# Small 64-row products that run over all 128 rows, and a mask product in float32r

## The chip, the core and the metric

The kernel runs on one core of one Trainium2 chip. The metric is the device time of one launch in microseconds (us), the median of three runs.

## What is computed

Two transformer blocks over one sequence of 512 tokens with 1024 features. All matrices are float32.

- First block, two layers: stick-breaking attention (16 heads of 64 features) and a squared-relu MLP; then retention (4 heads) and another such MLP; then a norm.
- Second block: a SwiGLU network, a mixer that runs two branches side by side, and a second SwiGLU network. One branch of the mixer is attention over the 128 keys that an index picks for each query (8 index heads and 8 attention heads of 64 features, two key/value heads). The other is an mLSTM (4 heads with queries and keys of 64 features).

Four kinds of product in it sum over just 64 features. The first of these lines is one of them, with the mask that belongs to it; the third is the index:

```
z = jnp.einsum('bhqd,bhkd->bhqk', qb, kp) * scale
mask = s_idx < t_idx
logits = jnp.einsum('bqhd,bsd->bqhs', iq_blk, ik)
```

## The kernel before

A float32 operand x is kept as two float32r tiles, hi and lo, with x = hi + lo; the class `Pair` holds the two. A product of two such operands is three TensorE products (`mm3`, lines 114 to 116): hi by lo, lo by hi, and hi by hi. Weights come from HBM in panels on SyncE's DMA queue; ScalarE rounds each to hi (line 197) and VectorE subtracts to get lo (line 198). Nearly every weight product moves 512 columns (the tokens).

Where the sum runs over 64 features, 64 rows of the array would stand empty, and `mm2` (lines 118 to 123) uses them. The stationary tile, `stack`, has hi of a head in one half of the 128 partitions and lo in the other. One product over all 128 rows then gives hi by hi and lo by hi at once (line 123, its moving tile has hi in both halves). What is missing is hi by lo, and line 122 makes it with a product over the 64 rows of hi alone: `stack[sl]` against `rhs.lo[sl]`, where `sl` is the head's half.

`mm2` is called in four places: `sb_z` (scores of stick-breaking attention, 64 calls), `select` (the index scores, 24), `attend_head` (attention scores, 32) and `weights` inside `mlstm` (16). That is 136 pairs of a 64-row and a 128-row product. They move 256, 384 or 512 columns.

The moving tiles are made in four places. `doubled` (line 142) makes them for the 16 stick-breaking heads, two heads at a time; the two heads share one lo tile, each has its own half. `ev` inside `mqk` (line 960) does the same for the mLSTM. The index keys (`ik_done`) and attention keys (`k_done`) already have lo in both halves.

In `sb_z` each score block also gets its mask from TensorE: a product of an identity and a constant `far` (-1e30 where the key is not before the query), 128 columns, added in PSUM (line 568). Both constants are bfloat16.

TensorE's order is woven: the generator `filler` yields weight products, and `pump` puts four `mm3` of them between two score blocks; in the mixer `weave` puts one step of the index, mLSTM or attention chain after every so many `mm3`. The instructions are then laid out by a scheduler, which may shift single ones. All tiles called h are taken from one heap of 70 buffers. VectorE, ScalarE and GpSimd (POOL) each run their own instructions in order. POOL does little: it clears the front columns of some tiles (lines 594 and 595) and cuts triangles (line 667).

Of the kernel before, what the change touches and what calls it, by code (L numbers as in the profile page):

```python
# [23 lines left out]
# tiles of the heap, buffers of the weights, and how far apart the woven chains put their steps  # L24
# [26 lines left out]
# pieces of the first panel  # L51
# [5 lines left out]
# [128, 512] views of one attention head's score blocks: (s-block, first t, columns in the bank)  # L57
# [6 lines left out]
# columns in front that hold only s > t  # L64
# [3 lines left out]
class Pair:  # L68
    """A float32 operand as two float32r tiles, x = hi + lo."""
# [8 lines left out]
class Builder:  # L78
# [39 lines left out]
    def mm2(self, ps, stack, rhs, sl, first, last):  # L118
        """Products over 64 partitions: stack holds hi in the partitions sl and lo in the other half, rhs is a
        Pair whose hi lies in both halves and whose lo lies (at least) in sl."""  # L120
        mm = self.nc.tensor.matmul
        mm(ps, stack[sl], rhs.lo[sl], start=first, stop=False)  # L122
        mm(ps, stack, rhs.hi, start=False, stop=last)  # L123

    def stack(self, f, scale=None):
        """[128, n], two heads of 64 features -> for each head a tile with hi in its half and lo in the other."""
# [15 lines left out]
    def doubled(self, f):  # L142
        """[128, n], two heads of 64 features -> for each head a Pair: hi in both halves, lo in its own."""
        nc = self.nc
        lo = self.h(F32R)
        out = []
        for b in range(2):
            t = self.h(F32R)
            a = slice(64 * b, 64 * b + 64)
            o = slice(64 - 64 * b, 128 - 64 * b)  # L150
            nc.scalar.activation(t[a], f[a], AF.Copy)
            nc.vector.tensor_tensor(lo[a], f[a], t[a].bitcast(F32), ALU.subtract)
            nc.vector.tensor_copy(t[o], t[a])
            out.append(Pair(t, lo))
        return out
# [8 lines left out]
    def panels(self, name, idxs):  # L164
        """Panels in the order of their use; each is one DMA and one or two subpanels."""
# [20 lines left out]
    def prep(self, ahead=AHEAD):  # L186
        """Split the next subpanel unless `ahead` of them wait already."""
# [15 lines left out]
    def next(self, name):  # L203
        """The next subpanel, a Pair."""
        assert self.subs[self.pos][0] == name, (self.subs[self.pos], name)
        while self.prep_at <= self.pos:
            self.prep(1)
        p = self.ready.pop(self.pos)
        self.pos += 1
        return p  # L210
# [11 lines left out]
    def g_tokens(self, name, X, done):  # L222
        """out [t, 512] = x W for the four token tiles; done(tt, psum)."""
# [11 lines left out]
    def g_tokens_turn(self, name, X, done):  # L235
        """The same, some token tiles after the other."""
# [12 lines left out]
    def later(self, f, *a, lag=None):  # L249
        """f(*a) after some more products."""  # L250
# [19 lines left out]
    def weave(self, main, chains=()):  # L270
        """Emit main's products, with a step of each chain [generator, period] every so many of them."""
# [9 lines left out]
    def rsqrt_col(self, v):  # L281
        """v -> v ** -0.5 for a few columns: three Newton steps from the exponent's half."""
# [12 lines left out]
    def spread(self, ps, cols, p=128):  # L295
        """cols(tt): [128, p] whose columns repeat (token on partition) -> ps [p, 512], token on the free axis."""
# [3 lines left out]
    def rows_of(self, ps, src, rhs, n=1, at=0, step=None, first=True, last=True):  # L300
        """Sums over src's partitions weighted by rhs [p, n], per token: ps[:, at + tt * step : + n]."""
# [17 lines left out]
    def mean_sq(self, box):  # L319
        """[128, 4] PSUM columns: sums of squares of the tokens."""  # L320
# [16 lines left out]
    def norm_soon(self, st, box, n1=N1, n2=N2):  # L337
        """Put the reciprocal norm into st["rcol"] and st["R"] while the first products run."""
# [8 lines left out]
    def gain_in(self, x, g):  # L347
        """hi/lo of x * g (g one value per partition)."""
# [7 lines left out]
    def setup(self):  # L356
# [9 lines left out]
        # ntri[j, s] = -1 where j >= s  # L366
# [6 lines left out]
        # far[s, c] = -1e30 where s >= c  # L373
# [4 lines left out]
        self.far = self.const("far", [128, 128], BF16)  # L378
        nc.vector.tensor_copy(self.far, far)
        # 1/64 within each half of the partitions  # L380
# [4 lines left out]
        # gains: one column per 128 features  # L385
# [9 lines left out]
    def mlp(self, layer, hh, X, box, nxt):  # L395
        """hh += relu(rms(hh) W_up)^2 W_down, X = hh * gain; calls nxt(m) when hh[m] is final."""
# [164 lines left out]
    def sb_z(self, q, k, head, ch, Z, i):  # L561
        sl = slice(64 * (head % 2), 64 * (head % 2) + 64)
        w = WIDTH[ch]
        z = self.ps("o" if ZB and i % 5 == 4 else "z")
        for j, t0, c0, c1 in CHUNKS[ch]:
            self.mm2(z[:, c0:c1], k[:, j * 128:(j + 1) * 128], q[:, t0:t0 + c1 - c0], sl, c0 == 0, False)
            d = c0 + j * 128 - t0
            self.nc.tensor.matmul(z[:, d:d + 128], self.identb, self.far, start=False, stop=c1 == w)
        Z[i] = z

    def sb_l1(self, Z, L, hc, i):
        """softplus(z), part one: ln(1 + exp(-|z|))."""
# [17 lines left out]
    def chunk(self, ch):  # L590
        """A Pair for a chunk, with zeros in the front columns."""
# [6 lines left out]
    def sb_tri(self, Z, L, A, hc, i):  # L598
        """z - sum of the softplus of the keys from s to t - 1, and its exponential."""
# [48 lines left out]
    def stack_values(self, vs, ps, scale):  # L648
        """[128, 512], eight heads of 64 -> two tiles of four heads, each 64 columns of hi and 64 of lo."""
# [7 lines left out]
    def mm_values(self, ps, v, a, first, last):  # L657
        """v [keys, 64 of hi, 64 of lo]: what v.lo brings lands in the partitions 64 to 127 of ps."""
# [4 lines left out]
    def keep(self, e, ch):  # L663
        """Zero where s > t."""
# [148 lines left out]
    def ffn(self, which, hh, X, st, nxt):  # L813
        """hh += (silu(x W_gate) * (x W_up)) W_down / 2, with x = X * st["R"]."""
# [17 lines left out]
        def main():  # L832
            for gi, grp in enumerate((range(0, 8), range(8, 16), range(16, 22))):
# [11 lines left out]
                if tail:  # L845
                    # the last tile in parts, so that little is left behind the last product
# [13 lines left out]
    def head_norm(self, x, gcol, done, p=128):  # L860
        """done(x [p, 512] * rsqrt(mean over each 64 partitions of x^2 + eps) * gcol), some products later."""
# [26 lines left out]
    def mixer(self, hh, X, box, nxt):  # L888
# [10 lines left out]
        # small projections: index key 0:64, input gate 64:68, index weights 68:76, forget gate 96:100  # L899
# [38 lines left out]
        # mLSTM operands  # L938
# [14 lines left out]
        def mqk():  # L953
            w = self.next("mqk")
            for h in range(4):
# [4 lines left out]
                def ev(ps=ps, h=h):  # L960
                    a = slice(64 * (h % 2), 64 * (h % 2) + 64)
                    o = slice(64 - 64 * (h % 2), 128 - 64 * (h % 2))
                    hi = self.h(F32R)
                    nc.scalar.activation(hi[a], ps[a], AF.Copy, scale=0.0625)
                    nc.scalar.activation(hi[o], ps[a], AF.Copy, scale=0.0625)
                    if h % 2 == 0:
                        MQ["lo"] = self.h(F32R)
                    lo = MQ["lo"]
# [40 lines left out]
        # attention operands  # L1009
# [131 lines left out]
    def topk_weights(self, gw):  # L1141
        """Index weights of tokens 128..511 as columns: [128, 24], eight to a query block."""
# [10 lines left out]
    def select(self, IQ, IK, late, BIAS):  # L1153
        """Attention bias [128, 512] of query blocks 1 to 3: 0 at the TOPK chosen keys, FAR elsewhere."""
# [5 lines left out]
        for tb in (1, 2, 3):  # L1160
            n = 128 * (tb + 1)
            sc = SC[tb] = self.h()
            for h in range(8):
                w = iw[:, (tb - 1) * 8 + h:(tb - 1) * 8 + h + 1]
                sl = slice(64 * (h % 2), 64 * (h % 2) + 64)
                ps = self.ps("z")
                self.mm2(ps[:, :n], IQ[h // 2][h % 2][:, tb * 128:(tb + 1) * 128], IK[:, 0:n], sl, True, True)
# [20 lines left out]
    def attend_all(self, AQ, KD, AV, BIAS, YA, choose, st):  # L1188
        """The eight heads' attention, query block by query block and group by group."""
# [23 lines left out]
    def attend_head(self, tb, g, hg, AQ, KD, BIAS, rq):  # L1213
# [5 lines left out]
        sl = slice(64 * (h % 2), 64 * (h % 2) + 64)  # L1219
        ps = self.ps("z")  # L1220
        self.mm2(ps[:, :w], AQ[h // 2][h % 2][:, tb * 128:(tb + 1) * 128], KD[g][:, 0:w], sl, True, True)
# [36 lines left out]
    def gates(self, gw, fgx, out):  # L1258
        """From the gate rows: exponent columns per (query block, key block), rows M, columns exp(-(F + M))."""
# [65 lines left out]
    def mlstm(self, MQ, MK, MV, gates, SO, YB):  # L1325
# [6 lines left out]
        # rows 32 h: sums of the weights, sums of num^2  # L1332
# [12 lines left out]
        def weights(h, ch):  # L1345
            o = slice(64 - 64 * (h % 2), 128 - 64 * (h % 2))
# [391 lines left out]
```

## Time and profile before

| | |
|---|---|
| median of three runs | 2569.13 us (2567.39 to 2570.67) |
| profiled execution, first to last instruction (span) | 2567.1 us |
| TensorE products busy (PE) | 2550.2 us, 99% of the span |
| TensorE weight loads busy (PEld, beside PE) | 2071.6 us, 81% |
| VectorE busy (DVE) | 1461.0 us, 57% |
| ScalarE busy (ACT) | 971.2 us, 38% |
| GpSimd busy (POOL) | 23.4 us, 1% |

The profile gives no time of its own for the profiled execution beside its span; the median of the runs is 2.0 us above that span. Products overlap in the records (one of 512 columns is shown 390 ns long, and the next one starts 230 ns after it), so the busy share of PE says that products follow each other without a break, and not how long one holds the array. That is read from the distance between starts. In the rows, "64*128 64x256" means that the stationary tile has 64 rows and 128 columns, and that 64 rows of 256 columns move.

### The profile page before, as it was taken

To read this page: it belongs to the slowest core of one execution; us is meant where nothing else is said; L and a number is where in the kernel's file an instruction comes from. 1 tells how busy PE (TensorE), PEld (TensorE's weight loads), DVE (VectorE), ACT (ScalarE), POOL (GpSimd) and SP (SyncE) were. 2 spreads that over 40 slices of the span, in tenths; PEclk is the share of its full clock that TensorE was granted. 3 is DMA by queue.
4 is the path that set the end of the run, shared out by engine and by line. 5 is a ranking of instruction groups with operands and counts; after the bars stand their busy time and mean duration, and the time that the engine had idled before them with its cause. 6 is when DMAs were issued, how large, how long until landed. Compare 5 with 4: busy or idle time off the path is not lost.

```text
span 2567.1 us, 28649 instructions
## 1 busy us (share of the span) xinstructions
PE 2550.2 (99%) x11511; PEld 2071.6 (81%) x11511; DVE 1461.0 (57%) x2386; ACT 971.2 (38%) x1428; POOL 23.4 (1%) x102
## 2 busy tenths in 40 slices
PE   9999999999999999999999999999999999999999
PEld 7777788888888888888888888888777778888887
DVE  7777754445555545645446644446788767543443
ACT  6676622223333323322223322223555454322221
POOL 0000000000000000000000000000000000000000
PEclk9999999999999999999999999999999999999999
DMA  4112022222222222222222222223121112222221
GB/s 166 57 42 99 33 99 99 99 99 99 94 85 85 86 82 103 79 94 92 97 99 99 96 93 91 99 90 107 63 82 66 61 55 82 99 99 98 93 86 68
DMA packets 35277, 225.58 MB, mean 88 GB/s; under 512 B 4036, under 2 KB 4420, under 8 KB 9800
## 3 DMA queue, kind: packets, MB, share of 16 engines
q1 hardware_dynamic: 34992, 223.69, 25.3%
q8 instruction: 91, 1.49, 0.2%
q14 instruction: 42, 0.34, 0.0%
q10 hardware_dynamic: 152, 0.06, 0.0%
HBM read 221.63 MB, written 2.10 MB: 87 GB/s over the span
## 4 chain that ended last, share of the span: by engine, by line
PE 97%; DVE 2%; ACT 1%; issue 1%; DMA 0%; SPq 0%; DVEq 0%
PE ps_m L114 28%; PE ps_m L115 28%; PE ps_m L116 28%; PE ps_z L122 2%; PE ps_z L123 2%; PE ps_z L116 1%; PE ps_z L114 1%; PE ps_z L115 1%; PE ps_z L614 1%; PE ps_z L615 1%; PE ps_o L298 1%; PE ps_o L305 1%; PE ps_m L660 0%; PE ps_m L661 0%; PE ps_z L886 0%
## 5 line engine op out<-in xcount | busy, mean ns | idle before, releaser
L114 PE MATMUL ps_m<-h,whi 128*128 128x512 f32 x3050 | 1195.4, 392 | 0.9 <-DVE h L920 0.4
L115 PE MATMUL ps_m<-h,wlo 128*128 128x512 f32 x3050 | 1189.1, 390 | 0.0
L116 PE MATMUL ps_m<-h,whi 128*128 128x512 f32 x3050 | 1188.2, 390 | 0.0
L197 ACT ACTIVATE whi<-raw 128x1024 fp32r<-128x1024 f32 (+2 forms) x417 | 437.5, 1049 | 1294.4 <-PE ps_m L116 1205.6
L116 PEld LDWEIGHTS ps_m<-h,whi 128*128 128x128 f32 x3050 | 573.4, 188 | 120.1
L114 PEld LDWEIGHTS ps_m<-h,whi 128*128 128x128 f32 x3050 | 573.9, 188 | 118.4 <-issue 3.1
L115 PEld LDWEIGHTS ps_m<-h,wlo 128*128 128x128 f32 x3050 | 573.7, 188 | 113.5 <-issue 1.2
L198 DVE TENSOR_TENSOR wlo<-raw,whi 128x1024 fp32r<-128x1024 f32 (+2 forms) x417 | 503.8, 1208 | 192.6 <-ACT whi L197 192.1
L159 ACT ACTIVATE h<-h 128x512 fp32r<-128x512 f32 (+1 forms) x172 | 107.9, 630 | 102.8 <-DVE h L405 27.7
L409 DVE TENSOR_TENSOR h<-h,ps_m 128x512 f32<-128x512 f32 x64 | 44.0, 687 | 170.4 <-PE ps_m L116 170.4
L160 DVE TENSOR_TENSOR h<-h 128x512 fp32r<-128x512 f32 (+1 forms) x172 | 116.3, 682 | 14.9 <-ACT h L159 14.2
L404 DVE TENSOR_TENSOR h<-ps_m,h 128x512 f32<-128x512 f32 x64 | 44.2, 691 | 139.3 <-PE ps_m L116 138.5
L823 DVE TENSOR_TENSOR h<-ps_m,h 128x512 f32<-128x512 f32 x43 | 29.7, 691 | 127.8 <-PE ps_m L116 127.8
L828 DVE SCALAR_TENSOR_TENSOR h<-ps_m,h 128x512 f32<-128x512 f32 x47 | 32.5, 692 | 118.9 <-PE ps_m L116 118.9
L820 DVE TENSOR_TENSOR h<-ps_m,h 128x512 f32<-128x512 f32 x42 | 29.0, 691 | 91.7 <-PE ps_m L116 91.1
L114 PE MATMUL ps_m<-wlo,h 128*128 128x512 f32 x176 | 70.2, 399 | 1.7 <-DVE wlo L198 1.7
L115 PE MATMUL ps_m<-whi,h 128*128 128x512 f32 x176 | 69.0, 392 | 0.0
L116 PE MATMUL ps_m<-whi,h 128*128 128x512 f32 x176 | 68.7, 391 | 0.0
L122 PE MATMUL ps_z<-h 64*128 64x256 f32 (+2 forms) x124 | 52.6, 427 | 2.2 <-ACT h L972 2.2
L122 PEld LDWEIGHTS ps_z<-h 64*128 64x128 f32 x124 | 22.6, 184 | 37.5 <-issue 21.7
L123 PE MATMUL ps_z<-h 128*128 128x256 f32 (+2 forms) x124 | 52.7, 429 | 0.0
L405 DVE SCALAR_TENSOR_TENSOR h<-h 128x512 f32<-128x512 f32 x64 | 44.3, 692 | 2.1
(286 smaller groups left out, 2028.9 us busy)
## 6 DMA issues: line engine op xcount, KB each, us to landing
raw<-gu SPq DMA_DIRECT2D x44, 1024.0 KB, 4.7
raw<-up SPq DMA_DIRECT2D x32, 1024.0 KB, 4.8
raw<-dn SPq DMA_DIRECT2D x32, 1024.0 KB, 4.8
raw<-fd SPq DMA_DIRECT2D x16, 1024.0 KB, 4.7
raw<-sbqk SPq DMA_DIRECT2D x8, 1024.0 KB, 4.8
raw<-retqk SPq DMA_DIRECT2D x8, 1024.0 KB, 4.7
raw<-retv SPq DMA_DIRECT2D x8, 1024.0 KB, 4.8
raw<-retg SPq DMA_DIRECT2D x8, 1024.0 KB, 4.8
```

What stands on the lines that cost most here:

```text
L114: mm(ps, lhs.hi, rhs.lo, start=first, stop=False, skip_group_check=skip)
L115: mm(ps, lhs.lo, rhs.hi, start=False, stop=False, skip_group_check=skip)
L116: mm(ps, lhs.hi, rhs.hi, start=False, stop=last, skip_group_check=skip)
L122: mm(ps, stack[sl], rhs.lo[sl], start=first, stop=False)
L123: mm(ps, stack, rhs.hi, start=False, stop=last)
L159: self.nc.scalar.activation(p.hi, x, AF.Copy)
L160: self.nc.vector.tensor_tensor(p.lo, x, p.hi.bitcast(F32), ALU.subtract)
L197: nc.scalar.activation(hi[:, a:b], r[:, a:b], AF.Copy)
L198: nc.vector.tensor_tensor(lo[:, a:b], r[:, a:b], hi[:, a:b].bitcast(F32), ALU.subtract)
L404: nc.vector.tensor_tensor(z, ps, st["R"], ALU.mult)
L405: nc.vector.scalar_tensor_tensor(z, z, 0.0, z, ALU.max, ALU.mult)
L409: nc.vector.tensor_tensor(hh[m], hh[m], ps, ALU.add)
```

## The change

1. `mm2` no longer takes the half `sl`: both products run over all 128 rows. For the first to give hi by lo alone, the moving lo tile is zero in the half where the stationary tile holds lo; where lo stood in both halves already (index keys, attention keys), the sum now has lo by lo as well.
2. `doubled` and `ev` in `mqk` make one lo tile for each head instead of one for two, and POOL clears its other half (20 new instructions in all: 16 for the stick-breaking heads, 4 for the mLSTM).
3. `far` and the identity of the mask product become float32r (the identity is now called `identr`).

Comments and docstrings are dropped as well, which shifts line numbers by a few: line 122 becomes 123, line 123 becomes 124, line 568 becomes 569.

```diff
-    def mm2(self, ps, stack, rhs, sl, first, last):
+    def mm2(self, ps, stack, rhs, first, last):
         mm = self.nc.tensor.matmul
-        mm(ps, stack[sl], rhs.lo[sl], start=first, stop=False)
+        mm(ps, stack, rhs.lo, start=first, stop=False)
         mm(ps, stack, rhs.hi, start=False, stop=last)
...
     def doubled(self, f):
         nc = self.nc
-        lo = self.h(F32R)
         out = []
         for b in range(2):
-            t = self.h(F32R)
+            t, lo = self.h(F32R), self.h(F32R)
             a = slice(64 * b, 64 * b + 64)
             o = slice(64 - 64 * b, 128 - 64 * b)
+            nc.gpsimd.memset(lo[o].bitcast(F32), 0.0)
             nc.scalar.activation(t[a], f[a], AF.Copy)
...
-        self.far = self.const("far", [128, 128], BF16)
+        self.far = self.const("far", [128, 128], F32R)
         nc.vector.tensor_copy(self.far, far)
...
-            self.mm2(z[:, c0:c1], k[:, j * 128:(j + 1) * 128], q[:, t0:t0 + c1 - c0], sl, c0 == 0, False)
+            self.mm2(z[:, c0:c1], k[:, j * 128:(j + 1) * 128], q[:, t0:t0 + c1 - c0], c0 == 0, False)
             d = c0 + j * 128 - t0
-            self.nc.tensor.matmul(z[:, d:d + 128], self.identb, self.far, start=False, stop=c1 == w)
+            self.nc.tensor.matmul(z[:, d:d + 128], self.identr, self.far, start=False, stop=c1 == w)
...
-                    hi = self.h(F32R)
+                    hi, lo = self.h(F32R), self.h(F32R)
+                    nc.gpsimd.memset(lo[a].bitcast(F32), 0.0)
                     nc.scalar.activation(hi[a], ps[a], AF.Copy, scale=0.0625)
                     nc.scalar.activation(hi[o], ps[a], AF.Copy, scale=0.0625)
-                    if h % 2 == 0:
-                        MQ["lo"] = self.h(F32R)
-                    lo = MQ["lo"]
...
-        self.identb = self.const("identb", [128, 128], BF16)
-        nc.vector.tensor_copy(self.identb, self.ident)
+        self.identr = self.const("identr", [128, 128], F32R)
+        nc.vector.tensor_copy(self.identr, self.ident)
```

The first score blocks of stick-breaking attention on TensorE, before (ps_z is the PSUM tile of a score block, whi and wlo are weights, the h tiles are heap buffers, brackets name the engines waited for):

```order
L115 MATMUL ps_m_459<-h_149,wlo_389 128x512
L122 MATMUL ps_z_452<-h_419,h_446 128x256 [waits Activation_49]
L116 MATMUL ps_m_459<-h_149,whi_388 128x512
...
L116 MATMUL ps_m_459<-h_153,whi_388 128x512
L122 MATMUL ps_z_489<-h_419,h_446 128x384
L123 MATMUL ps_z_452<-h_420,h_446 128x256 [waits DVE_49]
L568 LDWEIGHTS identb_115
L568 MATMUL ps_z_452<-far_86,identb_115 128x128
L122 MATMUL ps_z_452<-h_419,h_446 128x256
L123 MATMUL ps_z_452<-h_420,h_446 128x256
```

And now:

```order
L114 MATMUL ps_m_462<-h_162,whi_388 128x512
L115 MATMUL ps_m_462<-h_161,wlo_389 128x512
L123 MATMUL ps_z_455<-h_420,h_449 128x256 [waits DVE_49,Pool_49]
L124 MATMUL ps_z_455<-h_419,h_449 128x256
L569 MATMUL ps_z_455<-far_86,identr_115 128x128
L123 MATMUL ps_z_455<-h_420,h_449 128x256
L124 MATMUL ps_z_455<-h_419,h_449 128x256
L569 MATMUL ps_z_455<-far_86,identr_115 128x128
L123 MATMUL ps_z_492<-h_420,h_449 128x384
L124 MATMUL ps_z_492<-h_419,h_449 128x384
```

The first product of a pair no longer runs ahead between weight products, since it needs all of the stationary tile; it stands right ahead of the second one, and waits for VectorE and POOL where it waited for ScalarE. The mask product has no weight load of its own in the list any more.

POOL's instructions ahead of the mLSTM, before (lines 891 and 892 clear a mask tile, lines 1334 and 1335 clear two tiles of sums):

```order
L891 MEMSET h_12995 128x512 [waits DVE_49,PE_49,Pool_49]
L892 MEMSET h_12995 64x64 [waits Pool_49]
L1334 MEMSET h_13989 128x512 [waits DVE_49,PE_49]
L1335 MEMSET h_13990 128x512 [waits PE_49]
```

And now:

```order
L892 MEMSET h_13019 128x512 [waits DVE_49,PE_49,Pool_49]
L893 MEMSET h_13019 64x64 [waits Pool_49]
L965 MEMSET h_13969 64x512 [waits DVE_49,PE_49]
L965 MEMSET h_13981 64x512 [waits DVE_49,PE_49]
L965 MEMSET h_13993 64x512 [waits DMAHW6_49,DVE_49]
L965 MEMSET h_14005 64x512 [waits DVE_49]
L1331 MEMSET h_14019 128x512 [waits DVE_49,Pool_49]
L1332 MEMSET h_14020 128x512 [waits PE_49]
```

Four clears of a half tile stand in POOL's queue ahead of the two that were there; each waits for its heap buffer to come free.

## Rows read from the trace of the kernel before

**Rows 1.** The page: busy time, and the chain that ended last

```profile
PE 2550.2 (99%) x11511; PEld 2071.6 (81%) x11511; DVE 1461.0 (57%) x2386; ACT 971.2 (38%) x1428; POOL 23.4 (1%) x102
PE 97%; DVE 2%; ACT 1%; issue 1%; DMA 0%; SPq 0%; DVEq 0%
```

**Rows 2.** Timeline of PE, plain products: start us, length us, engine, line, tiles, shapes

```profile
200.29 0.28 PE L615 MATMUL ps_z<-h,nones 128*128 128x256 f32 x1
200.41 0.34 PE L614 MATMUL ps_z<-h,ntri 128*128 128x384 f32 x1
...
200.77 0.39 PE L114 MATMUL ps_m<-h,whi 128*128 128x512 f32 x1
201.00 0.40 PE L115 MATMUL ps_m<-h,wlo 128*128 128x512 f32 x1
```

**Rows 3.** Timeline of PE, a pair with 256 columns, in attention

```profile
2025.59 0.39 PE L116 MATMUL ps_m<-h,whi 128*128 128x512 f32 x1
2025.91 0.38 PE L122 MATMUL ps_z<-h 64*128 64x256 f32 x1
2026.22 0.38 PE L123 MATMUL ps_z<-h 128*128 128x256 f32 x1
...
2026.67 0.40 PE L115 MATMUL ps_m<-h,wlo 128*128 128x512 f32 x1
```

**Rows 4.** Timeline of PE, a pair with 384 columns and its mask

```profile
201.93 0.40 PE L116 MATMUL ps_m<-h,whi 128*128 128x512 f32 x1
202.25 0.44 PE L122 MATMUL ps_z<-h 64*128 64x384 f32 x1
202.62 0.44 PE L123 MATMUL ps_z<-h 128*128 128x384 f32 x1
202.90 0.23 PE L568 MATMUL ps_z<-far,identb 128*128 128x128 bf16 x1
...
203.26 0.40 PE L115 MATMUL ps_m<-h,wlo 128*128 128x512 f32 x1
```

**Rows 5.** Timeline of PE's weight loads (PEld): that of the 64-row product above

```profile
202.25 0.18 PEld L122 LDWEIGHTS ps_z<-h 64*128 64x128 f32 x1 [0.37 <-issue]
```

**Rows 6.** Timeline of PE, products over 4 rows in the mLSTM

```profile
1924.80 0.39 PE L116 MATMUL ps_m<-h,whi 128*128 128x512 f32 x1
1925.12 0.49 PE L1340 MATMUL ps_o<-h 4*128 4x512 f32 x1
...
1926.11 0.40 PE L115 MATMUL ps_m<-h,wlo 128*128 128x512 f32 x1
```

**Rows 7.** Instructions of lines 122 and 568: count, shortest/median/longest ns, first and last start

```profile
L122 PE MATMUL ps_z<-h x124: 286/435/579, 46.0 to 2122.6; 64*128 64x256 f32 x58, 64*128 64x384 f32 x33, 64*128 64x512 f32 x33
L122 PE MATMUL ps_o<-h x12: 379/408/497, 61.5 to 270.8; 64*128 64x256 f32 x6, 64*128 64x384 f32 x3, 64*128 64x512 f32 x3
L568 PEld LDWEIGHTS <-identb x64: 95/96/98, 48.0 to 287.3; 128*128 128x128 bf16 x64
```

**Rows 8.** Timeline of PE, four float32 products of 128 columns (two records each)

```profile
674.53 1.05 PE L298 MATMUL ps_o<-ident,c 128*128 128x128 f32 x8
...
675.66 0.39 PE L115 MATMUL ps_m<-h,wlo 128*128 128x512 f32 x1
```

**Rows 9.** Busy time by stretch: PE, PEld, DVE, ACT, POOL, granted clock, DMA share, GB/s

```profile
46.00:290.00 244.00, 243.85 (x1166) 187.32 (x1166) 179.82 (x304) 167.86 (x306) 11.29 (x55) 1.00 0.18 61
1845.00:1865.00 20.00, 20.00 (x90) 14.61 (x88) 18.48 (x47) 8.47 (x16) 0.00 (x0) 1.00 0.04 14
1845.00:1985.00 140.00, 137.47 (x575) 98.87 (x573) 123.47 (x265) 74.01 (x137) 6.94 (x21) 0.98 0.20 65
```

**Rows 10.** The same view for line 122 alone: PE, PEld, granted clock, DMA share, GB/s

```profile
1845.00:1985.00 140.00, 11.80 (x27) 4.89 (x27) 0.98 0.20 65
```

**Rows 11.** One of PE's waits: waited for, us in total, times, longest us

```profile
PE ps_z L122 <- ACT h L972: 2.2, 1, 2.2
```

**Rows 12.** A POOL clear among the groups: shapes, count, busy us, mean ns, idle before

```profile
L1334 POOL MEMSET h<- 128x512 f32 x1 | 0.5, 527 | 173.5 <-DVE h L1173 173.5
```

More of the change, by code (lines that the diff above doesn't have):

```diff
@@ L561, in sb_z @@
     def sb_z(self, q, k, head, ch, Z, i):
-        sl = slice(64 * (head % 2), 64 * (head % 2) + 64)
         w = WIDTH[ch]
@@ L1164, in select @@
                 w = iw[:, (tb - 1) * 8 + h:(tb - 1) * 8 + h + 1]
-                sl = slice(64 * (h % 2), 64 * (h % 2) + 64)
                 ps = self.ps("z")
-                self.mm2(ps[:, :n], IQ[h // 2][h % 2][:, tb * 128:(tb + 1) * 128], IK[:, 0:n], sl, True, True)
+                self.mm2(ps[:, :n], IQ[h // 2][h % 2][:, tb * 128:(tb + 1) * 128], IK[:, 0:n], True, True)
                 r = self.h()
@@ L1218, in attend_head @@
         h = 4 * g + hg
-        sl = slice(64 * (h % 2), 64 * (h % 2) + 64)
         ps = self.ps("z")
-        self.mm2(ps[:, :w], AQ[h // 2][h % 2][:, tb * 128:(tb + 1) * 128], KD[g][:, 0:w], sl, True, True)
+        self.mm2(ps[:, :w], AQ[h // 2][h % 2][:, tb * 128:(tb + 1) * 128], KD[g][:, 0:w], True, True)
         e = self.h()
@@ L1345, in weights @@
         def weights(h, ch):
-            o = slice(64 - 64 * (h % 2), 128 - 64 * (h % 2))
             q, k, mb = MQ[h], MK[h], MB[h]
@@ L1351, in weights @@
             for j, t0, c0, c1 in CHUNKS[ch]:
-                self.mm2(z[:, c0:c1], k[:, j * 128:(j + 1) * 128], q[:, t0:t0 + c1 - c0], o, c0 == 0, c1 == w)
+                self.mm2(z[:, c0:c1], k[:, j * 128:(j + 1) * 128], q[:, t0:t0 + c1 - c0], c0 == 0, c1 == w)
                 for tb in range(j, 4):
```

## The prediction

> **What bounds the kernel now.** The page first: products are busy for 2550.2 us of a span of 2567.1, and the chain that ended last is 97% PE [rows 1]. So a microsecond taken from TensorE's stream is a microsecond of the kernel, as long as VectorE and ScalarE keep up. But a busy PE may still do little, so the next view is the timeline of PE, read by the distance between starts. Plain float32r products go at 0.12 us for 256 columns (200.29 to 200.41), 0.18 for 384 (two of them from 200.41 to 200.77) and 0.23 for 512 [rows 2]. All these have 128 rows.
>
> A pair of `mm2` costs more than its columns. From L116 at 2025.59 to the second weight product behind the pair at 2026.67 are 1.08 us [rows 3]. In it lie L116, two products of 256 columns and L114: 0.23 + 0.12 + 0.12 + 0.23 = 0.70 at the steps above. The rest, 0.38 us, is lost. With 384 columns and the mask the stretch is 1.33 us (201.93 to 203.26) [rows 4]; plain steps give 0.23 + 0.18 + 0.18 + 0.23 = 0.82, so 0.51 are for the pair's loss and the mask. I split them as 0.38 and 0.13.
>
> Where is it lost? Ahead of the 64-row product the array comes 0.09 late (L116 to L122 0.32 instead of 0.23), and L122 to L123 takes 0.31 instead of 0.12 [rows 3]. The weight load of L122 starts at 202.25, together with its product, and not while L116 still runs [rows 5]. Is it the 64 rows, or something in these tiles? Products of another line with 4 rows show the same: from L116 at 1924.80 to L115 at 1926.11 are 1.31 us for four products of 512 columns [rows 6], 0.39 more than 4 x 0.23. So a change of the number of rows, to fewer and back, costs about 0.39 us in all: the weights of the first product on either side are not loaded under the product before it.
>
> **The change part by part.**
>
> *The rows.* Line 122 has 124 + 12 = 136 products [rows 7], and each stands between products of 128 rows. With 128 rows everywhere no change of rows is left but the mLSTM's 4-row ones. Columns and count of products stay, so 136 x 0.38 = 51.7 us go. Could 128 rows cost more than 64 for themselves? The steps of [rows 2] are for 128 rows already, and the sum above is made with them.
>
> One rule of the Trainium skill stands against this ("TensorE: Matmul & The Clock Gate", section "Why this matters for your kernels"): a product over few rows takes the same time as one over 128, and few rows gain only by running several at once. By it alone the first part would be worth nothing. The rows agree that a 64-row product is no shorter, but they show a loss around it that this rule does not name; it returns as a rival.
>
> *The mask.* 64 masks [rows 7] cost 0.13 us each now, 8.3 us. No row shows a float32r product of 128 columns; the narrowest has 256. Bounds: half of the 256-column step, 0.06, if nothing but its columns counted; and four float32 products of 128 columns, which with one product of 512 behind them take 1.13 us (674.53 to 675.66), so 0.90 / 4 = 0.225 each [rows 8]. Between them lies one of the two records of such a product, 0.11, which is what it would be if only the weight load of the next product counted. So the change is between 64 x -0.07 = -4.5 us and 64 x +0.095 = +6.1 us. I take the upper end: the float32 row is the nearest in width and in size of an element, and a fast rate at 256 columns does not show that 128 get it.
>
> The Trainium skill has a rule here too (same page, "Weight-path perf modes"): weights are loaded fast if there are 128 of them and their type is not float32. The trace agrees on the load itself: the bfloat16 one took 96 ns [rows 7], a float32r one 180 [rows 5]. By it alone 64 x 0.084 = 5.4 us would be added; I do not add it, since the 256 columns or more ahead of each mask are there to load under.
>
> *The clears.* 20 new POOL instructions of half a tile. A clear of a whole tile takes 0.53 us [rows 12], so at most 10.6 us on an engine that is busy for 23.4 of 2567.1 us [rows 1]. I cost them at nothing: their buffers are cleared long before the tile is filled. Without that cover the four of the mLSTM would stand in front of its first scores, where PE already waits 2.2 us for ScalarE's line 972 [rows 11]: 4 x 0.53 = 2.1 us.
>
> The heap gives one tile more for each two heads. The first pair now waits for VectorE and POOL, and runs as one piece, where line 122 ran ahead before; behind it only weight products are queued, and the masks' readers come later by a microsecond at most, once.
>
> *What is late next.* VectorE. In the stick-breaking stage (46 to 290 us) it is busy for 179.8 of 244 us [rows 9]. That stage has 64 pairs, so its time falls by 64 x 0.38 = 24.3 less 6.1, to 226 us, and the share rises from 74 to 80%: no bound, I take nothing. In the mixer it is close. From 1845 to 1985 VectorE is busy for 123.5 of 140 us [rows 9], and 27 of the 64-row products fall into it [rows 10] (10.3 us): 129.7 us would be left and VectorE would have to be busy for 95%. The densest stretch that I read in which PE never stood still is 1845 to 1865, with 18.48 of 20 us, 92.4% [rows 9]. At that share 123.5 us of work need 133.7 us, so 4.0 of the 10.3 us are given back there. Bounds: 0, and all 10.3.
>
> **The sum.** -51.7 + 6.1 + 0 + 4.0 = -41.6 us on the profiled span of 2567.1, that is 2525.5. The median of the runs lies 2.0 us above that span, and what lies around it does not change: 2527.5, say 2528 us.
>
> **The rivals.**
>
> 1. *The mask is as fast as its neighbours and VectorE keeps up.* Then -51.7 - 1.3 (0.11 instead of 0.13 for 64 masks) + 0 = -53: 2516 us. For it: float32r products of 256 to 512 columns keep one rate [rows 2], and the average of VectorE stays below 100%. Against it: the 92% above were reached beside no wait, but at 1907 PE already waited for the chain of VectorE and ScalarE [rows 11].
> 2. *VectorE takes over as the bound in the mixer and in the end of the stick-breaking stage.* The 24 index pairs and the 16 of the mLSTM are 15.2 us; if all of it is given back, and some 4 us more at the end of the first stage, where the chain from score to output has no weight products left to hide it, then -51.7 + 6.1 + 19 = -26.6: 2542 us. For it: VectorE's 88% there [rows 9]. Against it: its idle time in that stretch partly ends with PE's own products, and would shrink with them.
> 3. *The loss stays, so the kernel is slower.* If the 0.38 us belonged to these tiles and PSUM banks, or to the product after all as the skill's rule has it, the pairs would keep it and only the mask would change: +6.1 us, 2575 us. It decides if, in the new trace, L123 to L124 is still above 0.25 us for 256 columns. Against it: the 4-row products of other tiles lose the same [rows 6], and plain products into the same kind of PSUM tile lose nothing [rows 2].
> 4. *The change does not do what it says*, because narrow products stay between wide ones and the array changes its rows as often as before. Four pairs of 4-row products do stay in the mLSTM [rows 6], but alone and as before; they would have to sit beside most of the 136. Its time would be that of rival 3, and its chance is in there.
>
> **How the numbers follow.** My forecast, the mask at the float32 rate and some of the gain given back in the mixer: 0.50, own range 2520 to 2536. Rival 1: 0.28. Rival 2: 0.18. Rival 3: 0.03, with 0.01 for what I don't see. The range of 2512 to 2544 leaves out the slower case, the worst of rival 2 and a mask at its lowest bound. A difference of 0.2%, 5 us, is about what a measurement of this kernel can tell from no change. Faster by more needs only a tenth of the loss around the pairs to go: 0.95; within: 0.02; slower: 0.03.
>
> **What would show it.** In the changed trace: the step from L123 to L124 at 0.12, 0.18 and 0.23 us for 256, 384 and 512 columns, and 0.23 from L116 to L123; weight loads that start under the product before. The mask: line 569 with two records each, or a product behind it that is 0.2 us late, shows the float32 rate; 0.11 shows rival 1. The mixer between 1800 and 1970: PE's waits for VectorE (lines 920, 968, 972, 1173) grow from 2.5 us to about 6. The prediction is wrong if PE's waits there stay below 3 us, if the mask costs 0.13 or less, or if pairs still lose over 0.1 us.

## The result, and the profile after

The changed kernel takes 2525.2 us (2524.9 to 2526.0, 4 runs), the kernel before 2568.7 in the same session (2567.4 to 2570.7): 43.5 us less, a ratio of 0.9827 with a 95% interval of 0.9815 to 0.9839. The prediction was 2528, with 2512 to 2544 as its range.

The page of the changed kernel, its busy times and the chain that ended last; it answers to [rows 1]:

```profile
PE 2502.8 (99%) x11511; PEld 2075.6 (82%) x11511; DVE 1461.0 (58%) x2386; ACT 970.7 (38%) x1428; POOL 34.5 (1%) x122
PE 94%; DVE 3%; ACT 2%; issue 1%; DMA 0%; SPq 0%; ACTq 0%
```

As many products as before, 47.4 us less of them; VectorE and ScalarE have the same work, and POOL has 20 instructions and 11.1 us more. The chain is a little less PE and a little more VectorE and ScalarE than before.

The timeline of PE in the changed kernel, a pair with 256 columns in attention; it answers to [rows 3]:

```profile
1999.39 0.39 PE L116 MATMUL ps_m<-h,whi 128*128 128x512 f32 x1
1999.62 0.28 PE L123 MATMUL ps_z<-h 128*128 128x256 f32 x1
1999.73 0.28 PE L124 MATMUL ps_z<-h 128*128 128x256 f32 x1
1999.85 0.40 PE L114 MATMUL ps_m<-h,whi 128*128 128x512 f32 x1
2000.09 0.40 PE L115 MATMUL ps_m<-h,wlo 128*128 128x512 f32 x1
```

From 1999.39 to 2000.09 are 0.70 us, where it was 1.08: exactly the sum of the plain steps. The same view of a pair with 384 columns and its mask, which answers to [rows 4]:

```profile
187.63 0.40 PE L116 MATMUL ps_m<-h,whi 128*128 128x512 f32 x1
187.87 0.33 PE L123 MATMUL ps_z<-h 128*128 128x384 f32 x1
188.04 0.34 PE L124 MATMUL ps_z<-h 128*128 128x384 f32 x1
188.22 0.22 PE L569 MATMUL ps_z<-far,identr 128*128 128x128 f32 x1
188.28 0.45 PE L114 MATMUL ps_m<-h,whi 128*128 128x512 f32 x1
188.56 0.39 PE L115 MATMUL ps_m<-h,wlo 128*128 128x512 f32 x1
```

0.93 us where it was 1.33. The plain steps are 0.82, so the mask costs 0.11. And the weight loads there (PEld):

```profile
187.63 0.19 PEld L123 LDWEIGHTS ps_z<-h 128*128 128x128 f32 x1
...
188.04 0.19 PEld L569 LDWEIGHTS ps_z<-far,identr 128*128 128x128 f32 x1
188.22 0.19 PEld L114 LDWEIGHTS ps_m<-h,whi 128*128 128x128 f32 x1
188.33 0.19 PEld L115 LDWEIGHTS ps_m<-h,wlo 128*128 128x128 f32 x1
```

Each load now starts one product early: that of L123 at 187.63 together with L116. Before, L122's started with L122 [rows 5]. The mask is the one odd place: L114's load can start only at 188.22 with the mask, L115's at 188.33, and those 0.11 us are what the mask costs. Its own 128 columns are done before: L114's product starts 0.06 us behind the mask.

Where the time went is told by two stretches that hold the same products in both kernels, the stick-breaking stage and the mixer. Busy time by stretch, before (columns as in [rows 9]):

```profile
46.00:329.20 283.20, 278.65 (x1317) 215.47 (x1316) 211.44 (x362) 191.72 (x345) 11.29 (x55) 0.99 0.17 59
1815.00:2165.00 350.00, 347.36 (x1524) 256.77 (x1524) 279.06 (x657) 181.10 (x328) 8.42 (x26) 0.99 0.19 66
```

and after:

```profile
46.00:306.00 260.00, 253.75 (x1316) 216.51 (x1314) 212.25 (x362) 191.11 (x346) 18.12 (x68) 0.99 0.19 64
1792.00:2122.00 330.00, 324.03 (x1524) 258.98 (x1523) 278.05 (x657) 180.92 (x328) 10.66 (x30) 0.98 0.20 69
```

283.2 became 260.0, and 350.0 became 330.0: 23.2 and 20.0 us, together all of the 43.1 between the two spans (2567.1 and 2524.0). Nothing moved elsewhere. At 0.38 us a pair the 64 pairs of the first stage are worth 24.3 us, with 1.3 more for 64 masks at 0.11 instead of 0.13, and the 72 pairs of the mixer 27.4. So the first stage gave 2.4 us back and the mixer 7.4.

The clock moved the first of these. Before, the granted clock of TensorE fell from its full level (2.4 GHz) to half of it (1.2 GHz) twice in this stage, behind waits of 1.4 and 2.1 us (granted 0.57 on average from 294 to 298 and from 301 to 305 us); now it fell once, behind a wait of 2.1 us (0.57 from 279 to 283). One such stretch, 3.4 us long, costs 1.7 us, so without that the stage gave back 4.1. PE's waits in it grew from 4.3 to 5.9 us; the other 2.5 stay open.

PE's waits between 1815 and 2125 us in the changed kernel (who waits on whom, us in total, times, longest):

```profile
PE ps_m L114 <- DVE h L972: 3.5, 1, 3.5
PE ps_m L114 <- DVE h L921: 1.2, 1, 1.2
```

Before, the same place had the 2.2 us of [rows 11] and 0.4 more. With one more wait of 0.4 and three of 0.2 the changed kernel has 5.7 us against 2.6.

### The profile page after: what moved, and what is told of

Read it like the earlier page. It is cut to its first block, busy times and chain, and to the rows that moved or that the text cites. A ratio compares the mean times of both kernels' runs of the same rounds, so it can differ in the third digit from the quotient of the medians.

```text
span 2524.0 us, 28699 instructions
## 1 busy us (share of the span) xinstructions
PE 2502.8 (99%) x11511; PEld 2075.6 (82%) x11511; DVE 1461.0 (58%) x2386; ACT 970.7 (38%) x1428; POOL 34.5 (1%) x122
## 4 chain that ended last, share of the span: by engine, by line
PE 94%; DVE 3%; ACT 2%; issue 1%; DMA 0%; SPq 0%; ACTq 0%
PE ps_m L114 28%; PE ps_m L115 28%; PE ps_m L116 28%; PE ps_z L116 1%; PE ps_z L114 1%; PE ps_z L115 1%; DVE wlo L200 1%; PE ps_z L123 1%; PE ps_z L615 1%; PE ps_o L300 1%; PE ps_z L616 1%; PE ps_z L124 1%; PE ps_o L307 1%; ACT whi L199 0%; DMA raw<-sbv 0%
## 5 line engine op out<-in xcount | busy, mean ns | idle before, releaser
L114 PE MATMUL ps_m<-h,whi 128*128 128x512 f32 x3050 | 1194.8, 392 | 7.0 <-DVE h L972 3.5
L115 PE MATMUL ps_m<-h,wlo 128*128 128x512 f32 x3050 | 1189.3, 390 | 0.0
L116 PE MATMUL ps_m<-h,whi 128*128 128x512 f32 x3050 | 1188.1, 390 | 0.0
L114 PEld LDWEIGHTS ps_m<-h,whi 128*128 128x128 f32 x3050 | 573.5, 188 | 126.2 <-issue 6.6
L116 PEld LDWEIGHTS ps_m<-h,whi 128*128 128x128 f32 x3050 | 573.4, 188 | 119.4
L115 PEld LDWEIGHTS ps_m<-h,wlo 128*128 128x128 f32 x3050 | 573.9, 188 | 113.2 <-issue 1.2
L114 PE MATMUL ps_m<-wlo,h 128*128 128x512 f32 x176 | 70.3, 399 | 1.5 <-DVE wlo L200 1.0
L116 PE MATMUL ps_m<-whi,h 128*128 128x512 f32 x176 | 69.2, 393 | 0.0
L115 PE MATMUL ps_m<-whi,h 128*128 128x512 f32 x176 | 69.1, 392 | 0.0
L123 PE MATMUL ps_z<-h 128*128 128x256 f32 (+2 forms) x124 | 42.3, 342 | 0.1
L124 PE MATMUL ps_z<-h 128*128 128x256 f32 (+2 forms) x124 | 41.3, 334 | 0.0
L114 PEld LDWEIGHTS ps_m<-wlo,h 128*128 128x128 f32 x176 | 33.3, 189 | 8.3 <-DVE wlo L200 1.4
```

The source lines that it names most:

```text
L114: mm(ps, lhs.hi, rhs.lo, start=first, stop=False, skip_group_check=skip)
L115: mm(ps, lhs.lo, rhs.hi, start=False, stop=False, skip_group_check=skip)
L116: mm(ps, lhs.hi, rhs.hi, start=False, stop=last, skip_group_check=skip)
L123: mm(ps, stack, rhs.lo, start=first, stop=False)
```

## Experiments

Four questions were open: is the loss paid for each change of rows, what does a mask cost by itself, are the two stages' gains independent, and what takes back part of the mixer's.

**One part alone: the rows, with the mask in bfloat16.**

```diff
-        self.far = self.const("far", [128, 128], F32R)
+        self.far = self.const("far", [128, 128], BF16)
...
-        self.identr = self.const("identr", [128, 128], F32R)
+        self.identr = self.const("identr", [128, 128], BF16)
```

> The changed kernel with its mask constants in bfloat16 again, so that only the row part of the change is left. Theory A (a mask costs what the next product's weight load costs, 0.11 to 0.12 us, whatever its type; the 0.39 us around each 64-row product make the whole gain): same time as the changed kernel, 2525 us within 2. Rival B (the float32r mask costs 0.225 us, as the prediction had it, and the rows are worth more than was seen): faster than the changed kernel by 64 x 0.10 = 6 us, 2519.

2533.5 us, ratio to before 0.9859 (0.9846 to 0.9873). Neither theory had this: float32r is not dearer, it is worth 8 us. Its timeline has a mask in the same place:

```profile
191.37 0.39 PE L116 MATMUL ps_m<-h,whi 128*128 128x512 f32 x1
...
191.95 0.23 PE L569 MATMUL ps_z<-far,identr 128*128 128x128 bf16 x1
191.99 0.48 PE L114 MATMUL ps_m<-h,whi 128*128 128x512 f32 x1
192.31 0.40 PE L115 MATMUL ps_m<-h,wlo 128*128 128x512 f32 x1
```

0.94 us from 191.37 to 192.31, against 0.93. So 64 masks differ by about 1 us, and the rest must be elsewhere. PE's waits in the stick-breaking stage of this kernel, the longest of them:

```profile
PE ps_o L615 <- DVE h L586: 2.6, 1, 2.6
PE ps_m L661 <- DVE h L626: 2.1, 1, 2.1
PE ps_z L615 <- DVE h L586: 1.9, 3, 1.4
PE ps_z L615 <- DVE h L589: 1.2, 3, 0.7
```

They are 10.0 us in all; the changed kernel has 5.9 there, most of it in these:

```profile
PE ps_m L661 <- DVE h L626: 3.2, 2, 2.1
PE ps_m L114 <- DVE h L644: 1.4, 2, 0.9
```

New are the waits of L615, the running sums over keys, for the softplus of a block (L586, L589). Between the two profiled spans lie 5.8 us (2529.8 and 2524.0), so 4.1 us more of waits and about 1 for the masks are most of it. The scheduler lays the stage out anew when the mask's type changes, on VectorE too. That the type acts through this order was the new theory.

**The other part alone: the mask in float32r, in the kernel before.**

```diff
-        self.far = self.const("far", [128, 128], BF16)
+        self.far = self.const("far", [128, 128], F32R)
...
-        self.identb = self.const("identb", [128, 128], BF16)
+        self.identb = self.const("identb", [128, 128], F32R)
```

> The kernel before with its mask constants in float32r, so that only the mask part of the change is there. Theory A: no difference from before, 2569 us within 2, and the step from the mask to the second product behind it about the same as before. Rival B: slower than before by 6 us, 2575.

2566.9 us, ratio 0.9992 (0.9983 to 1.0001): no difference that can be told, and 6 us slower is excluded. Rival B falls.

**The cost per change of rows.**

```diff
         for j, t0, c0, c1 in CHUNKS[ch]:
-            self.mm2(z[:, c0:c1], k[:, j * 128:(j + 1) * 128], q[:, t0:t0 + c1 - c0], sl, c0 == 0, False)
+            mm(z[:, c0:c1], k[sl, j * 128:(j + 1) * 128], q.lo[sl, t0:t0 + c1 - c0], start=c0 == 0, stop=False)
+        for j, t0, c0, c1 in CHUNKS[ch]:
+            mm(z[:, c0:c1], k[:, j * 128:(j + 1) * 128], q.hi[:, t0:t0 + c1 - c0], start=False, stop=False)
             d = c0 + j * 128 - t0
```

> The kernel before with the order inside a stick-breaking score block changed: where a block has two parts (16 of the 48 blocks), both 64-row products come first, then the two 128-row ones with their masks. As many 64-row products as before, 136, but 118 stretches of them instead of 134. Theory A (the loss is paid for each change of rows and back): 16 x 0.39 = 6.2 us faster than before, 2562.5. Rival C (the loss belongs to each 64-row product, its tiles or its PSUM bank): no difference, 2569.

2563.4 us, ratio 0.9979 (0.9970 to 0.9989): 5.3 us faster, where 6.2 were expected and 0 by the rival. Its timeline shows the two 64-row products of a block as one row (line 567), between one change to 64 rows and one back:

```profile
57.09 0.39 PE L116 MATMUL ps_m<-h,whi 128*128 128x512 f32 x1
57.41 0.50 PE L567 MATMUL ps_z<-h 64*128 64x256 f32 x2
57.84 0.38 PE L569 MATMUL ps_z<-h 128*128 128x256 f32 x1
...
58.66 0.40 PE L115 MATMUL ps_m<-h,wlo 128*128 128x512 f32 x1
```

The same block in the kernel before, with two changes and two back:

```profile
56.11 0.39 PE L116 MATMUL ps_m<-h,whi 128*128 128x512 f32 x1
...
58.02 0.39 PE L115 MATMUL ps_m<-h,wlo 128*128 128x512 f32 x1
```

1.57 us against 1.91. Plain steps (0.94) and two masks at 0.13 make 1.20, so 0.37 are lost with one change and back, and 0.71 with two. 16 blocks at 0.34 are 5.4 us, the 5.3 measured. As many 64-row products over the same tiles and banks, fewer changes of rows, less time: the loss is paid per change.

**One stage alone.** The three callers of the mixer get a copy of the old `mm2`, with `stack[sl]` and `rhs.lo[sl]`, here for the index:

```diff
-                self.mm2(ps[:, :n], IQ[h // 2][h % 2][:, tb * 128:(tb + 1) * 128], IK[:, 0:n], True, True)
+                self.mm2half(ps[:, :n], IQ[h // 2][h % 2][:, tb * 128:(tb + 1) * 128], IK[:, 0:n], slice(64 * (h % 2), 64 * (h % 2) + 64), True, True)
```

> The changed kernel, but the mixer's three callers (index, attention, mLSTM: 72 products) run the first product of a pair over 64 rows again; clears and lo tiles stay as in the changed kernel. Theory A: 64 x 0.39 = 25 us of the stick-breaking stage stay, less 2 us of new waits on VectorE: 2546 us, 23 below before; and the mixer from its first index product to the end of attention takes as long as before, so the 8 us that the mixer gave back in the changed kernel come from VectorE being late there and not from the stick-breaking part. Rival D (the gain is one effect of the whole, for instance of the order that the scheduler chose): anything else than 2546 within 3.

2548.5 us, ratio 0.9918 (0.9905 to 0.9932): 20 us faster than before, 23 between the profiled spans (2567.1 and 2544.2), and its waits in the mixer are the 2.2 and 0.4 us of before. Theory A's 2546 within 3 holds. The two stages' gains add up, and what the mixer gives back begins with its own faster pairs.

**The price of a mask, doubled.**

```diff
-            self.nc.tensor.matmul(z[:, d:d + 128], self.identr, self.far, start=False, stop=c1 == w)
+            self.nc.tensor.matmul(z[:, d:d + 128], self.identr, self.far, start=False, stop=False)
+            self.nc.tensor.matmul(z[:, d:d + 128], self.identr, self.far, start=False, stop=c1 == w)
```

> The changed kernel with every float32r mask product made twice in a row (the mask then adds twice the same large negative number). Theory A (a mask costs the weight load behind it): the step from the first to the second mask is 0.11 us, 64 x 0.11 = 7 us slower than the changed kernel, 2532. Rival B (float32 rate below 256 columns): 0.21 to 0.225 us a mask, 14 us, 2539. In both PE's waits for VectorE may move by some us, because the scheduler lays out the stage anew; the step between two masks tells the theories apart whatever the waits do.

2533.1 us, 7.9 more than the changed kernel, where theory A had 7 and rival B 14. Its timeline:

```profile
191.03 0.39 PE L116 MATMUL ps_m<-h,whi 128*128 128x512 f32 x1
...
191.60 0.22 PE L569 MATMUL ps_z<-far,identr 128*128 128x128 f32 x1
191.66 0.28 PE L570 MATMUL ps_z<-far,identr 128*128 128x128 f32 x1
191.77 0.44 PE L114 MATMUL ps_m<-h,whi 128*128 128x512 f32 x1
192.05 0.39 PE L115 MATMUL ps_m<-h,wlo 128*128 128x512 f32 x1
```

1.02 us against 0.93: the second mask costs 0.09 to 0.10. The step between the starts of the two masks (0.06) is not that price; theory A's expectation had it at 0.11, and the 0.11 come one product later, in the step to L114. A single start-to-start step misleads here, the stretch between two plain products does not. At 64 x 0.10 the second masks are 6.4 of the 7.9 us; PE's waits in the stage grew by another 0.9. Products with hardly any columns say the same of the price: 12 float32 products of 2 columns, 24 records with a weight load each, take 2.77 us in one run (last section), 0.115 a record.

**The index work spread more thinly.**

```diff
-C1 = 8
+C1 = 12
```

> The changed kernel with the choice of the 128 keys (MAX8 and MATCH_REPLACE8 on VectorE) woven in at every 12th weight product instead of every 8th, from the mLSTM's value product on. Theory F (the mixer gives 8 us back because VectorE's backlog of index work delays lines 921 and 972 just when the mLSTM starts): PE's waits there, 1.2 and 3.5 us, shrink by 2 to 4 us, and 2521 to 2524 us come out. Rival G (the work must be done before attention anyway): attention waits for its bias instead, 2525 or slower.

2539.2 us, 14 slower than the changed kernel. The wait on line 972 stayed (3.9 us), and at 1996 PE waited 3.8 us for line 921, and at 2097 to 2109 3.5 us more. The clock fell to half its level behind these, for 3.4 us from 1996 and for 6.8 from 2098, which it does not do there in the changed kernel. Slower, as rival G had it; but the waits that grew are for lines 921 and 162, other work of VectorE, and not for the bias itself.

**The mLSTM's queries and keys earlier.**

```diff
+        self.weave(mqk(), [choose, gate])
         self.weave(units("mo", MO, mo_done), [choose, gate])
         self.weave(units("ga", G1, ga_done), [choose, gate])
-        self.weave(mqk(), [choose, gate])
```

> The changed kernel with the mLSTM's query and key product (four mm3, line 956) and its panel moved ahead of the output-gate and the first merge-gate products (32 mm3, 22 us of weight products), so that VectorE's lines 968 and 972 are issued that much before the mLSTM's first scores. Theory F: the wait of 3.5 us on line 972 goes, and with it the 6.8 us at half clock that follow it (3.4 us): 2518 to 2520 us. Rival H (VectorE's total work is the bound between 1840 and 1960): the wait only moves to other lines, and the time stays at 2525 within 1.5.

2526.0 us, as the changed kernel. The waits on line 972 moved along, to 1855 and 1860 us, 1.9 and 3.6 us long. Theory F had them gone. So they do not come from the mLSTM asking too early: the weight product that waits (L114, into ps_m) needs a PSUM bank that line 972 has still to read.

**The order of weight products alone.**

```diff
-FR = 0.5
+FR = 0.75
```

> The changed kernel with three quarters instead of half of the weight products of a stick-breaking step ahead of that step's VectorE work (the constant FR, 0.75 for 0.5). No product, tile or type differs. Theory I (what the mask's type moved was the order, and with it PE's waits for VectorE; a mask costs the same in either type): the stick-breaking stage changes by some us in either direction, say 2 to 8, by PE's waits, with the steps of the products as they were. Rival J (the order does not matter for this stage and the bfloat16 mask is dearer in a way the steps do not show): within 1 us of the changed kernel.

2525.8 us: inside 1 us, as rival J said. But it was a poor test of theory I: the scheduler put TensorE's products in another order and left VectorE's as it was, and the waits stayed the same to 0.1 us.

**The order on VectorE alone.**

```diff
-            if 0 <= i - 1 - DEPTH < NT:
-                self.sb_alo(A, order[i - 1 - DEPTH])
             if i < NT:
                 self.sb_l2(Z, L, order[i], i)
+            if 0 <= i - 1 - DEPTH < NT:
+                self.sb_alo(A, order[i - 1 - DEPTH])
```

> The changed kernel with the stick-breaking step's lo half of the weights of an earlier block (line 626) written behind that step's softplus work (lines 586 to 589) instead of ahead of it: the same instructions on every engine, in another order on VectorE. Theory I (the 8 us between the two mask types came from the order on VectorE and PE's waits, not from the mask's price): the stage from 46 to 326 us changes by 1 to 8 us either way, by PE's waits, with a mask at 0.11 to 0.12 as before. Rival J (that order does not matter): within 1 us of the changed kernel.

2531.1 us, 5.9 slower than the changed kernel, with a mask at the same step. Waits of L615 for L586 and L589 appear as with the bfloat16 mask, 2.2 and 2.0 us in ps_z:

```profile
PE ps_z L615 <- DVE h L589: 2.2, 4, 0.9
PE ps_z L615 <- DVE h L586: 2.0, 3, 1.1
```

The order on VectorE alone is worth 5.9 us where the mask's type was worth 8.3. That the 8 us of the first experiment are this effect is likely, not shown: both types in one fixed order was not tried.

**VectorE unloaded in the mixer**, in the changed kernel and in the kernel before:

```diff
-                nc.vector.max(m, sc[:, :n])
-                nc.vector.match_replace(sc[:, :n], m, sc[:, :n], DROP)
+                if r == 0:
+                    nc.vector.max(m, sc[:, :n])
+                    nc.vector.match_replace(sc[:, :n], m, sc[:, :n], DROP)
                 yield
```

> The changed kernel with 15 of the 16 rounds of MAX8 and MATCH_REPLACE8 left out for each query block (45 pairs in all, 8 keys are chosen instead of 128; the rest of the weave stays), about 48 us of VectorE work less in the mixer. Theory F (VectorE's backlog gives back 8 of the mixer's 28 us): PE's waits on VectorE between 1840 and 1960 us all but vanish, no stretch at half clock is left there, and 2516 to 2519 us come out. Rival K (the missing 8 us are lost in the products themselves, not in waits): 2523 to 2525.

> The kernel before with the same work left out. Theory F: its own wait of 2.2 us and the half clock behind it go, 2563 to 2566 us; the difference from the changed kernel without that work is then 50 us, near the full 136 x 0.38 = 52, against 43.5 with VectorE loaded. Rival K: the difference stays 43 to 45 us.

2523.1 us, 2.1 less than with the work; and 2570.2 for the kernel before, where 2568.9 were measured beside it with the work: no difference that can be told. Between the two lie 47.1 us, and 44.2 between their profiled spans (2566.1 and 2521.9), not 50; rival K was nearer. In the stretch from 1870 to 1960 VectorE's busy time fell from 82.48 (changed kernel) to 52.36 us (without the choice), the rows in this order:

```profile
1870.00:1960.00 90.00, 84.69 (x390) 64.71 (x389) 82.48 (x167) 58.97 (x115) 8.01 (x25) 0.96 0.21 71
```

```profile
1870.00:1960.00 90.00, 87.37 (x401) 66.44 (x400) 52.36 (x91) 58.70 (x115) 9.50 (x25) 0.95 0.19 66
```

Yet the wait on line 972 is still there, in the kernel without the choice:

```profile
PE ps_m L114 <- DVE h L972: 2.6, 2, 2.2
```

The wait on line 921 (1.2 us) is gone and that on line 972 is 0.9 shorter: these are the 2.1 us. What is left is the chain behind each `mqk` product, three ScalarE and two VectorE instructions that hold its PSUM bank until line 972 has read it. It stands in VectorE's queue among other work. In the changed kernel:

```profile
1872.90 0.59 ACT L967 ACTIVATE h<-ps_m 64x512 fp32r<-64x512 f32 x1
...
1874.36 1.22 DVE L200 TENSOR_TENSOR wlo<-raw,whi 128x1024 fp32r<-128x1024 f32 x1
1875.61 0.68 DVE L968 SCALAR_TENSOR_TENSOR h<-ps_m,h 64x512 fp32r<-64x512 f32 x1
...
1877.51 0.69 DVE L972 SCALAR_TENSOR_TENSOR h<-ps_m,h 64x512 fp32r<-64x512 f32 x1
```

ScalarE is done with line 967 at 1873.49, and line 968 runs only at 1875.61, behind line 921, line 1171 and the weight split of line 200; VectorE was busy for 3.90 of the 4.00 us from 1873 to 1877. From the chain's first instruction to its last are 5.9 us here (1872.31 to 1878.20), and 4.1 without the choice (1871.09 to 1875.17), with line 200 still ahead of line 968. So the queue has a part in this wait even where VectorE's share is 58%. No run here shortened the chain itself.

**VectorE's weight split on POOL.**

```diff
+            e = nc.gpsimd if name in ("mo", "ga", "akv", "aq") and self.prep_at % 2 == 0 else nc.vector
-            nc.vector.tensor_tensor(lo[:, a:b], r[:, a:b], hi[:, a:b].bitcast(F32), ALU.subtract)
+            e.tensor_tensor(lo[:, a:b], r[:, a:b], hi[:, a:b].bitcast(F32), ALU.subtract)
```

> The changed kernel with the subtraction that makes the lo half of a weight panel (line 200, 1.2 us on VectorE) on POOL for every second subpanel of four of the mixer's weights (output gate, first merge gate, attention keys and values, queries). Theory F: some 10 us of VectorE work leave its busiest stretch, the waits on lines 921 and 972 shrink, 2518 to 2522 us. Rival L (POOL is too slow at it, or slows VectorE's own accesses, or PE waits for the panel instead): 2525 or slower.

2530.6 us, 5.4 slower than the changed kernel: rival L. The wait on the chain's end grew to 4.0 us. POOL took 2.41 us for the subtraction that takes VectorE 1.22, and VectorE's own line 1171 took 0.85 us on average over 512 columns in the mixer where it takes 0.74; how much of the 5.4 us each of rival L's reasons made is open. None of the kernels that do the whole work beats the changed one.

## Why the prediction was right

**The rows: right, and nearly to size.** The step said that the loss around each pair goes and that plain steps remain. The traces show 0.70 where it was 1.08, the grouped kernel shows that the loss is paid per change of rows, and the two stages gave 23.2 and 20.0 of 24.3 and 27.4 us. The prediction counted 136 changes; the trace of before has 134, since two pairs of 64-row products in the mixer touch. Rival 3 falls: the loss went with the 64 rows. The rule of the Trainium skill behind it ("TensorE: Matmul & The Clock Gate", section "Why this matters for your kernels") is that a product over few rows takes the same time as one over 128. The trace agrees for the product itself: the second 64-row product of a grouped block adds no loss of its own (0.37 us for the block, where one pair alone loses 0.38). The change around it is what costs.

**The mask: the term that was mis-sized.** The prediction took "the upper end", +6.1 us, from the float32 products of [rows 8]. Measured: 0.11 us a mask, 0.09 to 0.10 for a second one, about 1 us less than before for all 64. The prediction had named "0.13 or less" as a sign that it is wrong, and by this sign its step for the mask failed; rival 1 had this part right. The prediction took the float32 product of the same width for the nearest row. What came out is the mark between its bounds, one record of such a product (0.11): the weight load of the product behind, which a mask of 128 columns is too short to cover, in bfloat16 as in float32r (0.94 and 0.93 us for the same stretch). The Trainium skill's rule on fast weight loads ("TensorE: Matmul & The Clock Gate", section "Weight-path perf modes") is that weights load fast if there are 128 of them and their type is not float32. The load records agree (96 ns for bfloat16, 188 ns for float32r). The longer load costs nothing here, because it lies under the 256 columns or more ahead, as the prediction said.

**The mixer: right in sign, wrong in cause.** 4.0 us were to be given back because VectorE would have to be busy for 95%, and PE's waits there were to grow from 2.5 us to about 6. They grew from 2.6 to 5.7, and 7.4 us were given back. The 3.1 us of waits are one part. The two changes that were counted too many are 0.8. A second stretch at half clock, 3.4 us long (below), is another 1.7; the other 1.8 stand in no list of waits and stay open. The step that failed is the ceiling of 92.4% for VectorE. In the changed kernel it was busy for 96% of 50 us while PE hardly stood still (busy time of PE first, of VectorE third):

```profile
1820.00:1870.00 50.00, 49.78 (x226) 40.22 (x225) 48.01 (x110) 23.97 (x39) 2.62 (x5) 1.00 0.20 69
```

And 30 us less work for VectorE in its busy stretch won 2.1 us. A stretch's busy share says when an engine could be the bound; here PE waited for a chain across two engines that holds PSUM banks, with other work of VectorE between its links.

**The sum.** Two errors went against each other: the mask was 7.4 us too dear (+6.1 for -1.3), and what is given back was 5.9 us too cheap (4.0 for 9.9 in both stages). So the forecast of 2525.5 us for the span came within 1.5 of the measured 2524.0 partly by luck; with the mask at 0.11 the same working would have given 2518.1.

**The clears** cost nothing that shows: 16 and 4 of them, 8.6 and 2.1 us of POOL, and no wait of PE on POOL is in the lists of the two stages.

## What to carry to other kernels

On a busy TensorE, read distances between starts from one plain product to the next plain one, over whatever lies between: a change in the number of rows and back shows as 0.38 us there, and as 0.09 to 0.19 in any single step. A product with idle rows is worth filling with zeros when it stands alone between full ones, or worth grouping with its like. And price a short product by the weight load behind it before looking at its type. When a type changes, compare the order of the other engines too: here the scheduler moved VectorE's work, and that this made the 8 us is likely, not shown.

## What was not expected of the hardware

**A clock that falls, or not, behind the same run.** Both kernels issue 12 float32 products of 2 columns (24 records, two each) for the query norms in one run. Before:

```profile
1989.84 2.77 PE L305 MATMUL ps_o<-half,h 128*128 128x2 f32 x24
```

and in the changed kernel:

```profile
1955.54 2.84 PE L307 MATMUL ps_o<-half,h 128*128 128x2 f32 x24 [0.17 <-ACT h L1387]
```

Before, the granted clock stayed at its full level (2.4 GHz) behind them. In the changed kernel it fell to the half level (1.2 GHz), here from 1959.00 on (granted clock third from the end):

```profile
1955.00:1959.00 4.00, 3.83 (x29) 3.37 (x28) 3.58 (x8) 3.95 (x8) 0.59 (x2) 0.98 0.02 4
1959.00:1962.40 3.40, 3.40 (x11) 2.62 (x10) 2.04 (x3) 1.26 (x3) 0.41 (x2) 0.52 0.00 0
```

PE is shown busy for 3.83 of 4 us ahead of the fall, with one wait of 0.17, and 11 products go at half speed behind it. All fourteen profiled executions of this study have this run. In six PE waited for 0.16 to 0.22 us just ahead of it, and each time the clock fell with it or behind it. In the other eight there was no such wait, and the clock fell in one of them, the changed kernel without the choice. What decides it is open; breaking up the run was not tried.

One profile is one execution. In 20 executions of the kernel before, the mean granted clock was between 0.995 and 0.999 and the time between 2573.9 and 2566.2 us, longer where the clock was lower.

**float32r at 128 columns** costs no more than the next weight load in this stream, 0.10 to 0.11 us, half of what a float32 product of that width takes [rows 8], and the same as bfloat16.
